# The scan of an RWKV-7 layer: a step's values with the direction outermost, and two neighbouring chunks side by side in the blocks of L

## Chip and metric

One core of a Trainium2 chip runs the whole program, one launch. The metric is the device time of one execution in microseconds; it is given as the median of three runs. Engines are named as in the profile: PE (TensorE), DVE (VectorE), ACT (ScalarE), POOL (GpSimd) and SP (SyncE), from whose queue nearly all DMAs are issued.

## What is computed

Two layers of a diffusion backbone over 512 latent and 256 context tokens with 1024 channels. The change lies in layer 1, whose mixer is a bidirectional RWKV-7: 16 heads of 64 channels, each with a 64 x 64 state that is carried along the tokens once forwards and once backwards, first over the context, then over the latent tokens.

```python
def wkv_scan(r, w, kk, bvec, k, v, s0, reverse):
    def step(s, inp):
        r_t, w_t, kk_t, b_t, k_t, v_t = inp
        sk = jnp.einsum('bhvk,bhk->bhv', s, kk_t)
        s = s * w_t[:, :, None, :] - sk[..., None] * b_t[:, :, None, :] + v_t[..., None] * k_t[:, :, None, :]
        return s, jnp.einsum('bhvk,bhk->bhv', s, r_t)
    ...
for d, rev in enumerate((False, True)):
    s_c, y_c = wkv_scan(rc, dc[d][0], kkc, dc[d][1], dc[d][2], vc, s0, rev)
    _, y_l = wkv_scan(rl, dl[d][0], kkl, dl[d][1], dl[d][2], vl, s_c, rev)
```

## The kernel before

The tokens are cut into 12 chunks of 64 (8 latent, 4 context). The kernel works chunk by chunk: within a chunk the recurrence is solved with a 64 x 64 triangular matrix L per head and direction, whose inverse is applied to the right-hand sides, and only the state passes from chunk to chunk. A step `i` of the scan (`tm_scan`, 12 steps) takes one chunk of the forward direction and one of the backward direction, listed in `order`: forwards the chunk number rises by one from step to step, backwards it falls by one. The two directions lie in the two halves of the 128 partitions (`half`), so nearly every load of the scan fills 64 partitions. Heads are counted as 8 tiles `kt` of 2 heads `n`.

Before the scan, `tm_prep` has written to HBM the keys (`kbd`), queries (`qld`, `qcd`) and the blocks of L (`ld`, with 64 columns a chunk, all 12 chunks of a row side by side), and `tm_values` the values (`vd`, one row of 4 KB per token).

`tm_feed(i)` loads what step `i` needs: four loads of keys KB (256 KB each), two of queries QZ (512 KB each, 256 KB for context), and two of values W (256 KB each, one per direction, L1071). It then makes G = QZ x KB on PE, masks it on DVE (L1082), and transposes KB on PE (L1096). `tm_feed(i + 1)` is a generator of which one part runs after each `kt` of step `i`. KB has room for one step only, so the next KB loads wait for the transposes; QZ and W have room for two steps.

`tm_invert(j)` serves steps 2j and 2j + 1: it loads their blocks of L into the tile XT (four loads of 256 KB, L1111), copies the triangles into GL with a mask (four copies, L1114, DVE), transposes GL into Z (L1118) and inverts the 32 x 32 blocks by a row of small products on DVE or POOL (L1124, L1125). `tm_below(j)` transposes the result into XN and XD (L1133, L1134) and completes the inverse on PE; ACT writes it back into XT in place (L1148, L1156). XT has three buffers, so pairs 0, 1 and 2 are loaded before the scan and pairs 3, 4 and 5 when an earlier pair has been used, at the ends of steps 1, 3 and 5.

`tm_step(i, kt)` multiplies W with G, applies the inverse from XT, writes the solution into W through a mask (L1182), and multiplies it with the transposed keys into the new state S (L1194). After four `kt` the state is copied into the W of the next step (L1200).

Each engine works its instructions in order, and so does each DMA queue. The order is not that of the code: the program is built with `TileContext(nc, schedule_with_timeline_sim=True)`, a planner that places each engine's instructions by estimates of their durations and adds the waits between engines by which parts of a tile they read and write. After the scan `out1_ahead` uses buffers of XT for weights (L1359).

Of the kernel before, what the change touches and what calls it, by code (L numbers as in the profile page):

```python
# [7 lines left out]
F32 = mybir.dt.float32  # L8
F32R = mybir.dt.float32r
I32 = mybir.dt.int32  # L10
AF = mybir.ActivationFunctionType
# [4 lines left out]
P = 128  # L16
D = 1024
KT = 8
# [16 lines left out]
class Net:  # L35
# [1014 lines left out]
    half = staticmethod(lambda n: slice(64 * n, 64 * n + 64))  # L1050

    def tm_feed(self, i, KB=None, W=None):

        nc, half = self.nc, self.half
        f = self.feeds[i] = {}
        cs = self.order[i]
        lat = cs[0] < 8
        m = 128 if lat else 64
        KB = KB or [self.sb([P, 4, 2, 128], F32, "KB", 2) for _ in range(2)]
        W = f["W"] = W or self.sb([P, KT, 2, 2, 64], F32, "W", 2)  # L1060
        QZ = f["QZ"] = self.QZ[i % 2]
        by = lambda z: z.rearrange("k (n p) m -> p (k n) m", n=2)
        flat = lambda z: z.rearrange("p k n m -> p (k n) m")
        for d in range(2):
            h = half(1 - d)
            for g in range(2):
                nc.sync.dma_start(flat(KB[g][h]), by(self.kbd[d, 4 * g:4 * g + 4, :, cs[d]]))
            nc.sync.dma_start(flat(QZ[h, :, :, d, 0:m]), by(self.qld[d, :, :, cs[d]] if lat else self.qcd[d, :, :, cs[d] - 8]))
        for d in range(2):
            v = self.vd[64 * cs[d]:64 * cs[d] + 64].rearrange("t (k n v) -> t k n v", n=2, v=64)  # L1070
            nc.sync.dma_start(W[half(d), :, d], v)  # L1071
        f["G"], f["KT"] = [], []
        yield
        for g in range(4):
            ps = self.mm2()
            for j in range(2):
                for n in range(2):
                    x = 2 * m * (2 * j + n)
                    self.mm(ps[:, x:x + 2 * m], KB[g // 2][:, 2 * (g % 2) + j, n], QZ[:, 2 * g + j, n, :, 0:m], True, True)
            G = self.sb([P, 2, 2, 2, m], F32, "G", 8)  # L1080
            f["G"].append(G)
            nc.vector.tensor_mul(G.rearrange("p k n d t -> p (k n) d t"),  # L1082
                                 ps[:, :8 * m].rearrange("p (k d t) -> p k d t", d=2, t=m),
                                 self.gmask[:, :, 0:m].unsqueeze(1).to_broadcast([P, 4, 2, m]))
            if i:

                for d in range(2):
                    h = half(1 - d)
                    nc.scalar.activation(G[h, :, :, d, 0:64], QZ[h, 2 * g:2 * g + 2, :, d, 0:64], AF.Copy)
            yield  # L1090
        for g in range(2):
            ps = self.mm2()
            for j in range(4):
                for n in range(2):
                    x = 256 * j + 128 * n
                    nc.tensor.transpose(ps[:, x:x + 128], KB[g][:, j, n], self.ident)  # L1096
            T = self.sb([P, 4, 2, 128], F32, "KT", 3, pool=self.gp)
            nc.scalar.activation(T, ps.rearrange("p (k n x) -> p k n x", k=4, n=2), AF.Copy)
            f["KT"].append(T)
            yield  # L1100

    def tm_invert(self, j):


        nc = self.nc
        XT = self.XT[j] = self.sb([P, 2, 2, KT, 64], F32, "XT", 3, pool=self.ip)
        for s in range(2):
            for d in range(2):
                c = self.order[2 * j + s][d]
                h = self.half(1 - d)  # L1110
                nc.sync.dma_start(XT[h, s].rearrange("p n k t -> p (n k) t"),  # L1111
                                  self.ld[:, :, h, 64 * c:64 * c + 64].rearrange("n k p t -> p (n k) t"))
            for b in range(2):
                nc.vector.copy_predicated(self.GL[:, 16 * s:16 * s + 16],  # L1114
                                          self.pmask[:, b].unsqueeze(1).to_broadcast([P, 16, 32]),
                                          XT[:, s, :, :, 32 * b:32 * b + 32].rearrange("p n k t -> p (n k) t"))
        Z = self.Z[j] = self.sb([P, 32, 32], F32, "Z", 2, pool=self.ip)
        nc.vector.transpose(Z, self.GL.rearrange("p u t -> p t u"))  # L1118
        zt = self.sb([P, 256], F32, "zt", 2)
        eng = nc.gpsimd if j in self.pool_inverse else nc.vector  # L1120
        for u in range(1, 31):
            n = 31 - u
            t = zt[:, 0:n * u].rearrange("p (a b) -> p a b", b=u)
            eng.tensor_mul(t, Z[:, u + 1:, u:u + 1].to_broadcast([P, n, u]), Z[:, u:u + 1, 0:u].to_broadcast([P, n, u]))  # L1124
            eng.tensor_add(Z[:, u + 1:, 0:u], Z[:, u + 1:, 0:u], t)  # L1125

    def tm_below(self, j):

        nc, Z = self.nc, self.Z[j]
        XA = self.XT[j]  # L1130
        XT = XA.rearrange("p s n k t -> p (s n k) t")
        XD, XN = (self.sb([P, 32, 32], F32, n, 1, pool=self.ip) for n in ("XD", "XN"))
        nc.vector.transpose(XN.rearrange("p u t -> p t u"), Z.rearrange("p t s -> p s t"))  # L1133
        nc.vector.transpose(XD.rearrange("p u t -> p t u"), Z)  # L1134
        units = lambda z: z.rearrange("p (n k) t -> p n k t", n=2)
        for s in range(2):
            us = slice(16 * s, 16 * s + 16)
            pp = self.mm2()[:, :512].rearrange("p (u t) -> p u t", t=32)
            for u in range(16):
                for h in (0, 64):  # L1140
                    self.mm(pp[h + 32:h + 64, u], XT[h:h + 32, 16 * s + u, 32:64], XN[h:h + 32, 16 * s + u], True, True)
            PL = self.sb([P, 16, 32], F32, "PL", 2, pool=self.ip)
            for h in (32, 96):
                nc.scalar.activation(PL[h:h + 32], pp[h:h + 32], AF.Copy)
            for d, z in ((0, XD), (1, XN)):
                h = self.half(1 - d)
                for b in range(2):
                    nc.scalar.activation(XA[h, s, :, :, 32 * b:32 * b + 32], units(z[h, us]), AF.Copy, scale=self.bmask[h, b:b + 1])  # L1148
            yield
            pp = self.mm2()[:, :512].rearrange("p (u t) -> p u t", t=32)  # L1150
            for u in range(16):
                for h, d in ((0, 1), (64, 0)):
                    x, y = PL[h + 32:h + 64, u], XD[h + 32:h + 64, 16 * s + u]
                    self.mm(pp[h + 32 * d:h + 32 * d + 32, u], *((y, x) if d else (x, y)), True, True)
            for d, h in ((0, 64), (1, 32)):
                nc.scalar.activation(XA[h:h + 32, s, :, :, 32 - 32 * d:64 - 32 * d], units(pp[h:h + 32]), AF.Copy)  # L1156
            yield

    def tm_step(self, i, kt):

        nc, half, order = self.nc, self.half, self.order
        f, cs = self.feeds[i], order[i]
        lat, first, last = cs[0] < 8, i == 0, i == len(order) - 1
        g, j = kt // 4, kt % 4
        W = f["W"][:, kt]
        XT = self.XT[i // 2][:, i % 2]
        Q = f["QZ"][:, kt]
        G = f["G"][kt // 2][:, kt % 2]
        K = f["KT"][g][:, j]
# [1 line left out]
        units = [(d, n) for n in range(2) for d in range(2)]  # L1171
# [6 lines left out]
        nc.scalar.activation(rh, pr[:, 0:128].rearrange("p (n v) -> p n v", n=2), AF.Copy)  # L1178
        for d, n in units:
            h = half(1 - d)  # L1180
            self.mm(pr[h, col(1, n)], XT[h, n, kt], rh[h, n], True, True)
        nc.vector.copy_predicated(W, self.umask.unsqueeze(2).unsqueeze(3).to_broadcast([P, 2, 2, 64]),  # L1182
                                  pr[:, 128:256].rearrange("p (n v) -> p n v", n=2).unsqueeze(1).to_broadcast([P, 2, 2, 64]))
        if not last:
# [11 lines left out]
            if j == 3:  # L1196
                W2 = self.feeds[i + 1]["W"]
                for d in range(2):
                    h = half(1 - d)
                    nc.scalar.activation(W2[h, 4 * g:4 * g + 4, d], self.S2[h], AF.Copy)  # L1200
            if j == 3 and i < len(order) - 2:
                m = self.dec[:, :, 4 * g:4 * g + 4, i + 1].rearrange("p n k -> p k n")
                self.Sd[g] = self.sb([P, 4, 2, 64], F32, "Sd", 3, pool=self.gp)
# [72 lines left out]
    def tm_scan(self):  # L1276
# [5 lines left out]

        qz = lambda j: self.sb([P, KT, 2, 2, 128], F32, "QZ%d" % j)
        q = qz(0)
        ahead = [self.sb([P, 4, 2, 128], F32, "KB", 2) for _ in range(2)], self.sb([P, KT, 2, 2, 64], F32, "W", 2)
        self.QZ = [q, qz(1)]
        for j, z in enumerate(self.QZ):
            for d in range(2):
# [2 lines left out]
        n, below = len(self.order), iter(())  # L1291
# [56 lines left out]
    def out1_ahead(self):  # L1348

        nc, a = self.nc, self.a  # L1350
        gs = self.sb([P, 32, 32], F32, "Z", 2, pool=self.ip).rearrange("p a b -> p (a b)")
        nc.sync.dma_start(gs, a["rw_gup"])
        st = [self.sb([P, 2, 2, KT, 64], F32, "XT", 3, pool=self.ip) for _ in range(2)]
        self.ahead = gs, [z.rearrange("p a b c d -> p (a b c d)").rearrange("p (k n) -> p k n", n=256) for z in st]
        for c in range(2):
            self.load_wo(self.ahead[1][c], c)
# [171 lines left out]
```

## Time and profile before

| | us |
|---|---|
| median of 3 runs | 2261.82 |
| lowest and highest of the runs | 2259.23, 2261.92 |
| the profiled execution | 2269.31 |
| its span, first to last instruction | 2267.5 |

The profile is of one execution, all of whose times are counted from the first instruction of its span. The scan with the inversions ahead of it lies between about 1375 and 1820 us. The page gives the engines' shares; the views by stretch, the waits and the timelines go into single stages. In a row, `XT<-ldr` is a load of the tile XT from the HBM tensor ldr, and `mm<-QZ,KB` a product of QZ and KB into a PSUM tile. A packet is one piece of a DMA on one of 16 DMA engines.

### The profile page before, as it was taken

The numbers are of one execution on the slowest core, as the hardware profiler recorded it, in microseconds if no ns is written. First come the engines' busy times: TensorE is split into PE (matmuls) and PEld (weight loads), VectorE is DVE, ScalarE is ACT, GpSimd is POOL, SyncE is SP. The second block draws the span as 40 slices with busy tenths as digits, with TensorE's granted clock in tenths as the row PEclk, the third lists the DMA queues.
The fourth block names the chain that finished last, engine by engine and source line by source line (L and its number), as shares of the span: only waits on it lengthen the run. The fifth ranks groups of instructions, "written<-read, shape, count | busy, mean of one in ns | idle before, by whom it ended". The sixth has DMA issues, their size and how long they took to land. (4 is left out here: it accounts for less than half of the span.)

```text
span 2267.5 us, 37320 instructions
## 1 busy us (share of the span) xinstructions
PE 2023.4 (89%) x15710; PEld 1619.3 (71%) x15710; DVE 1145.4 (51%) x1835; ACT 869.6 (38%) x1333; POOL 519.6 (23%) x530
## 2 busy tenths in 40 slices
PE   5888889999999999997987769779787778999999
PEld 3666547778888888875765449667676666888887
DVE  4556664342222222328647997648575684333333
ACT  3664454231121221317744543346454432232321
POOL 0122331010010100105004983661500220110110
PEclk8999999999999999998998778889898999999999
DMA  7324441123333122212224659396644440222222
GB/s 282 119 86 136 143 164 41 37 94 119 124 129 113 56 64 67 98 42 79 93 88 148 236 223 214 71 143 102 113 91 80 76 140 19 93 93 93 93 93 93
DMA packets 231944, 248.93 MB, mean 110 GB/s; under 512 B 52448, under 2 KB 209504, under 8 KB 225376
## 3 DMA queue, kind: packets, MB, share of 16 engines
q1 hardware_dynamic: 229728, 241.30, 36.8%
q0 software_dynamic: 896, 3.15, 0.4%
q8 instruction: 123, 2.02, 0.4%
q10 hardware_dynamic: 1152, 2.10, 0.2%
q14 instruction: 45, 0.37, 0.1%
HBM read 200.82 MB, written 41.94 MB: 107 GB/s over the span
## 5 line engine op out<-in xcount | busy, mean ns | idle before, releaser
L264 ACT ACTIVATE whi<-wst 128x1024 fp32r<-128x1024 f32 x160 | 169.2, 1059 | 587.3 <-PE mm L47 567.0
L47 PE MATMUL mm<-hhi,whi 128*128 128x512 f32 (+1 forms) x992 | 346.8, 356 | 16.2 <-ACT hhi L250 6.7
L47 PE MATMUL mm<-hlo,whi 128*128 128x512 f32 (+1 forms) x992 | 352.0, 356 | 3.6 <-DVE hlo L251 3.4
L47 PE MATMUL mm<-hhi,wlo 128*128 128x512 f32 (+1 forms) x992 | 349.6, 353 | 0.0
L265 DVE TENSOR_TENSOR wlo<-wst,whi 128x1024 fp32r<-128x1024 f32 x160 | 199.9, 1251 | 255.2 <-ACT whi L264 252.4
L345 POOL TENSOR_TENSOR mp<-mr 128x768 f32<-128x768 f32 (+1 forms) x64 | 109.9, 1719 | 848.1 <-ACT mr L344 848.1
L47 PE MATMUL mm<-ahi,wlo 128*128 128x512 f32 (+1 forms) x704 | 252.9, 359 | 0.0
L47 PE MATMUL mm<-ahi,whi 128*128 128x512 f32 (+1 forms) x704 | 252.9, 360 | 0.0
L47 PE MATMUL mm<-alo,whi 128*128 128x512 f32 (+1 forms) x704 | 252.5, 359 | 0.0
L300 DVE SCALAR_TENSOR_TENSOR Xt<-mm,mod,Xt 128x512 f32<-128x512 f32 (+1 forms) x112 | 70.6, 653 | 336.8 <-PE mm L47 336.6
L47 PEld LDWEIGHTS mm<-hhi,whi 128*128 128x128 f32 x992 | 187.8, 191 | 55.2 <-ACT hhi L250 8.7
L47 PEld LDWEIGHTS mm<-hlo,whi 128*128 128x128 f32 x992 | 188.9, 190 | 32.1 <-DVE hlo L251 6.6
L47 PEld LDWEIGHTS mm<-hhi,wlo 128*128 128x128 f32 x992 | 188.4, 190 | 28.3 <-issue 0.8
L47 PEld LDWEIGHTS mm<-ahi,whi 128*128 128x128 f32 x704 | 132.2, 188 | 28.1 <-issue 6.7
L47 PEld LDWEIGHTS mm<-ahi,wlo 128*128 128x128 f32 x704 | 132.5, 188 | 22.0 <-DVE wlo L265 1.1
L47 PEld LDWEIGHTS mm<-alo,whi 128*128 128x128 f32 x704 | 132.4, 188 | 21.9
L47 PE MATMUL mm<-QZ,KB 128*128 128x256 f32 (+1 forms) x384 | 96.4, 408 | 48.1 <-DMA QZ<-qlr 20.3
L47 PEld LDWEIGHTS mm<-QZ,KB 128*128 128x128 f32 x384 | 74.1, 227 | 60.3 <-issue 26.3
L347 DVE TENSOR_TENSOR alo<-mp,ahi 128x768 fp32r<-128x768 f32 (+1 forms) x64 | 54.9, 858 | 113.1 <-ACT ahi L346 113.0
L1082 DVE TENSOR_TENSOR G<-mm,gmask 128x1024 f32<-128x1024 f32 (+1 forms) x48 | 50.2, 1047 | 88.1 <-PE mm L47 87.8
L346 ACT ACTIVATE ahi<-mp 128x768 fp32r<-128x768 f32 (+1 forms) x64 | 47.3, 739 | 110.3 <-POOL mp L345 110.3
L47 PE MATMUL sc<-W,G 128*64 128x64 f32 (+1 forms) x1280 | 67.8, 233 | 12.8 <-DVE S L1194 10.3
(462 smaller groups left out, 4207.7 us busy)
## 6 DMA issues: line engine op xcount, KB each, us to landing
wst<-in_mlp_w_dram SPq DMA_DIRECT2D x64, 1024.0 KB, 5.4
wst<-in_ada_w_dram SPq DMA_DIRECT2D x48, 1024.0 KB, 6.4
kbr<-KB SPq DMA_DIRECT2D x16, 768.0 KB, 4.5
KB<-kbr SPq DMA_DIRECT2D x48, 256.0 KB, 5.6
wst<-in_rw_w_rkv_dram SPq DMA_DIRECT2D x8, 1024.0 KB, 5.4
qlr<-ql SPq DMA_DIRECT2D x16, 512.0 KB, 3.3
QZ<-qlr SPq DMA_DIRECT2D x16, 512.0 KB, 8.8
wst<-in_hy_w_in_dram SPq DMA_DIRECT2D x7, 1024.0 KB, 5.3
```

Of the source, the lines that this page charges most:

```text
L47: self.nc.tensor.matmul(out, lhsT, rhs, start=start, stop=stop)
L264: nc.scalar.activation(hi, w, AF.Copy)
L265: nc.vector.tensor_sub(lo, w, hi.bitcast(F32))
L300: self.nc.vector.scalar_tensor_tensor(x, ps[:, c0:c1], self.m(l, chunk, v, kt), x, op0=OP.mult, op1=OP.add)
L345: nc.gpsimd.tensor_mul(p[:, :n], r[:, :n], r[:, :n])
L346: nc.scalar.activation(h[:, :n], p[:, :n], AF.Copy)
L347: nc.vector.tensor_sub(o[:, :n], p[:, :n], h[:, :n].bitcast(F32))
L1082: nc.vector.tensor_mul(G.rearrange("p k n d t -> p (k n) d t"), ps[:, :8 * m].rearrange("p (k d t) -> p k d t", d=2, t=m), self.gmask[:, : ...
```

## The change

W has its axes as direction, `kt`, head, value in place of `kt`, direction, head, value. A direction's values of one token are then 4 KB in one piece in the tile as well as in HBM, where the load before had 8 pieces of 512 B.

XT has its axes as head, `kt`, chunk of the pair, column in place of chunk, head, `kt`, column. A pair's two chunks are neighbours in HBM, so one load per direction brings both, in pieces of 128 columns (512 B) in place of 64 (256 B): two loads of 512 KB in place of four of 256 KB. Place `s` in a tile is now the lower or higher chunk rather than the earlier or later step: the earlier step finds its chunk at place 0 for the forward and at place 1 for the backward direction (`at`). The four copies into GL each read a place of both loads. The instructions on the engines are the same in number and size; their strides differ. The tiles are as large as before.

```diff
@@ tm_feed
-        W = f["W"] = W or self.sb([P, KT, 2, 2, 64], F32, "W", 2)
+        W = f["W"] = W or self.sb([P, 2, KT, 2, 64], F32, "W", 2)
         for d in range(2):
-            v = self.vd[64 * cs[d]:64 * cs[d] + 64].rearrange("t (k n v) -> t k n v", n=2, v=64)
-            nc.sync.dma_start(W[half(d), :, d], v)
+            nc.sync.dma_start(W[half(d), d].rearrange("p k n v -> p (k n v)"), self.vd[64 * cs[d]:64 * cs[d] + 64])
@@ tm_invert
-        XT = self.XT[j] = self.sb([P, 2, 2, KT, 64], F32, "XT", 3, pool=self.ip)
+        XT = self.XT[j] = self.sb([P, 2, KT, 2, 64], F32, "XT", 3, pool=self.ip)
+        for d in range(2):
+            c = min(self.order[2 * j][d], self.order[2 * j + 1][d])
+            h = self.half(1 - d)
+            nc.sync.dma_start(XT[h].rearrange("p n k s t -> p (n k) (s t)"),
+                              self.ld[:, :, h, 64 * c:64 * c + 128].rearrange("n k p t -> p (n k) t"))
         for s in range(2):
-            for d in range(2):
-                c = self.order[2 * j + s][d]
-                h = self.half(1 - d)
-                nc.sync.dma_start(XT[h, s].rearrange("p n k t -> p (n k) t"),
-                                  self.ld[:, :, h, 64 * c:64 * c + 64].rearrange("n k p t -> p (n k) t"))
             for b in range(2):
                 nc.vector.copy_predicated(self.GL[:, 16 * s:16 * s + 16],
                                           self.pmask[:, b].unsqueeze(1).to_broadcast([P, 16, 32]),
-                                          XT[:, s, :, :, 32 * b:32 * b + 32].rearrange("p n k t -> p (n k) t"))
+                                          XT[:, :, :, s, 32 * b:32 * b + 32].rearrange("p n k t -> p (n k) t"))
@@ tm_below
-            us = slice(16 * s, 16 * s + 16)
+            at = s, 1 - s
...
-                    nc.scalar.activation(XA[h, s, :, :, 32 * b:32 * b + 32], units(z[h, us]), AF.Copy, scale=self.bmask[h, b:b + 1])
+                    nc.scalar.activation(XA[h, :, :, at[d], 32 * b:32 * b + 32], units(z[h, 16 * at[d]:16 * at[d] + 16]), AF.Copy,
+                                         scale=self.bmask[h, b:b + 1])
...
@@ tm_step
-        W = f["W"][:, kt]
-        XT = self.XT[i // 2][:, i % 2]
+        W = f["W"][:, :, kt]
+        XT = [self.XT[i // 2][:, :, :, (i + d) % 2] for d in range(2)]
...
-                    nc.scalar.activation(W2[h, 4 * g:4 * g + 4, d], self.S2[h], AF.Copy)
+                    nc.scalar.activation(W2[h, d, 4 * g:4 * g + 4], self.S2[h], AF.Copy)
```

## Rows read from the trace of the kernel before

**Rows 1.** the page: busy time, share of the span, instructions of PE
```profile
PE 2023.4 (89%) x15710; PEld 1619.3 (71%) x15710; DVE 1145.4 (51%) x1835; ACT 869.6 (38%) x1333; POOL 519.6 (23%) x530
```

**Rows 2.** stretches: length, busy us per engine, clock, DMA share, GB/s
```profile
1375.00:1464.00 89.00, 73.42 (x801) 72.24 (x801) 64.32 (x87) 22.17 (x30) 45.55 (x70) 0.89 0.56 116
1464.00:1820.00 356.00, 287.45 (x5315) 244.24 (x5314) 221.65 (x552) 173.16 (x369) 106.96 (x152) 0.89 0.60 103
```

**Rows 3.** waits, 1464 to 1820: total us, times, longest
```profile
PE mm L47 <- DMA QZ<-qlr: 20.3, 4, 7.8
...
DVE GL L1114 <- DMA XT<-ldr: 14.5, 5, 5.3
...
PE mm L47 <- DMA KB<-kbr: 6.8, 4, 2.8
```

**Rows 4.** timeline of PE: start, us, instruction, [idle before, what ended it]
```profile
1441.53 0.69 PE L47 MATMUL mm<-XN,XT 32*32 32x32 f32 x18 [14.27 <-DVE XN L1133]
...
1523.74 1.62 PE L47 MATMUL mm<-QZ,KB 128*128 128x128 f32 x6 [0.28 <-DMA KB<-kbr]
...
1542.64 1.19 PE L47 MATMUL mm<-QZ,KB 128*128 128x256 f32 x2 [2.81 <-DMA KB<-kbr]
...
1635.73 0.58 PE L47 MATMUL sc<-W,G 128*64 128x64 f32 x5 [4.53 <-DVE S L1194]
...
1743.28 0.79 PE L47 MATMUL mm<-QZ,KB 128*128 128x256 f32 x1 [7.80 <-DMA QZ<-qlr]
...
1778.28 1.19 PE L47 MATMUL mm<-QZ,KB 128*128 128x256 f32 x2 [8.10 <-issue]
```

**Rows 5.** timeline of SP's queue: start and us of the issues
```profile
1379.14 9.71 SPq L1111 DMA_DIRECT2D XT<-ldr  x7
...
1511.76 1.50 SPq L1111 DMA_DIRECT2D XT<-ldr  x2
1513.37 4.49 SPq L1067 DMA_DIRECT2D KB<-kbr  x2
...
1731.12 0.52 SPq L1071 DMA_DIRECT2D W<-vdr  x1
1731.73 1.74 SPq L1068 DMA_DIRECT2D QZ<-qlr  x2
...
1767.64 3.06 SPq L1067 DMA_DIRECT2D KB<-kbr  x2
```

**Rows 6.** timeline of DVE: the copies into GL
```profile
1383.24 1.52 DVE L1114 COPY_PREDICATED GL<-pmask,XT 128x512 f32<-128x512 int32 x2 [4.35 <-DMA XT<-ldr]
1387.88 1.52 DVE L1114 COPY_PREDICATED GL<-pmask,XT 128x512 f32<-128x512 int32 x2 [3.12 <-DMA XT<-ldr]
...
1634.59 0.73 DVE L1114 COPY_PREDICATED GL<-pmask,XT 128x512 f32<-128x512 int32 x1 [5.32 <-DMA XT<-ldr]
...
1645.93 0.73 DVE L1114 COPY_PREDICATED GL<-pmask,XT 128x512 f32<-128x512 int32 x1 [4.17 <-DMA XT<-ldr]
```

**Rows 7.** DMA, 1728 to 1745: packets, MB, share of 16 engines
```profile
q1 hardware_dynamic: 5248, 2.62, 92.2%
```

**Rows 8.** DMA, 1380 to 1389, XT loads
```profile
q1 hardware_dynamic: 5172, 1.30, 93.4%
```

**Rows 9.** DMA, 1030.8 to 1035, one load into 128 partitions; GB/s by slice
```profile
GB/s 0 0 0 0 0 0 0 0 0 0 93 171 215 180 88 39 73 34 24 68 190 351 327 351 351 351 351 341 356 346 332 225 102 29 5 0 0 0 0 0
...
q1 hardware_dynamic: 1040, 0.52, 41.9%
```

**Rows 10.** DMA, 1511.0 to 1511.3: issues, KB, us to landing
```profile
QZ<-qlr SPq DMA_DIRECT2D x1, 512.0 KB, 5.5
```

**Rows 11.** tile XT: count, ns min/median/max, first and last start
```profile
L1148 ACT ACTIVATE XT<-XN,bmask x24: 704/722/725, 1441.6 to 1788.0; 64x512 f32<-64x512 f32 x24
```

**Rows 12.** tile bo, 1816 to 1822
```profile
L1233 SPq DMA_DIRECT2D bo<-vdr x4: 524/628/970, 1816.3 to 1818.6; - x4
...
DMA to landing us min/median/max: 2.6/2.9/3.1
```

More of the change, by code (lines that the diff above doesn't have):

```diff
@@ L1130, in tm_below @@
         XA = self.XT[j]
-        XT = XA.rearrange("p s n k t -> p (s n k) t")
+        XT = XA.rearrange("p n k s t -> p (n k) s t")
         XD, XN = (self.sb([P, 32, 32], F32, n, 1, pool=self.ip) for n in ("XD", "XN"))
@@ L1136, in tm_below @@
         for s in range(2):
-            us = slice(16 * s, 16 * s + 16)
+            at = s, 1 - s
             pp = self.mm2()[:, :512].rearrange("p (u t) -> p u t", t=32)
             for u in range(16):
-                for h in (0, 64):
-                    self.mm(pp[h + 32:h + 64, u], XT[h:h + 32, 16 * s + u, 32:64], XN[h:h + 32, 16 * s + u], True, True)
+                for h, d in ((0, 1), (64, 0)):
+                    self.mm(pp[h + 32:h + 64, u], XT[h:h + 32, u, at[d], 32:64], XN[h:h + 32, 16 * at[d] + u], True, True)
             PL = self.sb([P, 16, 32], F32, "PL", 2, pool=self.ip)
@@ L1152, in tm_below @@
                 for h, d in ((0, 1), (64, 0)):
-                    x, y = PL[h + 32:h + 64, u], XD[h + 32:h + 64, 16 * s + u]
+                    x, y = PL[h + 32:h + 64, u], XD[h + 32:h + 64, 16 * at[d] + u]
                     self.mm(pp[h + 32 * d:h + 32 * d + 32, u], *((y, x) if d else (x, y)), True, True)
             for d, h in ((0, 64), (1, 32)):
-                nc.scalar.activation(XA[h:h + 32, s, :, :, 32 - 32 * d:64 - 32 * d], units(pp[h:h + 32]), AF.Copy)
+                nc.scalar.activation(XA[h:h + 32, :, :, at[d], 32 - 32 * d:64 - 32 * d], units(pp[h:h + 32]), AF.Copy)
             yield
@@ L1180, in tm_step @@
             h = half(1 - d)
-            self.mm(pr[h, col(1, n)], XT[h, n, kt], rh[h, n], True, True)
+            self.mm(pr[h, col(1, n)], XT[d][h, n, kt], rh[h, n], True, True)
         nc.vector.copy_predicated(W, self.umask.unsqueeze(2).unsqueeze(3).to_broadcast([P, 2, 2, 64]),
@@ L1284, in tm_scan @@
         q = qz(0)
-        ahead = [self.sb([P, 4, 2, 128], F32, "KB", 2) for _ in range(2)], self.sb([P, KT, 2, 2, 64], F32, "W", 2)
+        ahead = [self.sb([P, 4, 2, 128], F32, "KB", 2) for _ in range(2)], self.sb([P, 2, KT, 2, 64], F32, "W", 2)
         self.QZ = [q, qz(1)]
@@ L1352, in out1_ahead @@
         nc.sync.dma_start(gs, a["rw_gup"])
-        st = [self.sb([P, 2, 2, KT, 64], F32, "XT", 3, pool=self.ip) for _ in range(2)]
+        st = [self.sb([P, 2, KT, 2, 64], F32, "XT", 3, pool=self.ip) for _ in range(2)]
         self.ahead = gs, [z.rearrange("p a b c d -> p (a b c d)").rearrange("p (k n) -> p k n", n=256) for z in st]
```

## The prediction

> **What bounds the kernel now.** I read the page first: PE is busy for 89% of the span [rows 1], so only a stage in which PE waits can be changed much by loads. The table by stretches finds it: from 1464 to 1820 us (the scan) PE is busy 287 of 356 us, and in the 89 us before it (values and first inversions) 73 of 89 [rows 2]. Everything that the diff touches lies in these two stretches. The list of waits in the scan names what PE and DVE sit idle for: the loads QZ 20.3 us, KB 6.8 us, and, on DVE, XT 14.5 us [rows 3]. The loads of W themselves hardly appear; they matter by standing in SP's queue ahead of QZ, KB and XT. The timeline of PE then shows single waits: 14.27 us for XN before the scan, and inside it 2.81 us where a step's KB load comes first in the queue, 7.80 us where QZ comes last, 8.10 us where KB comes last [rows 4]. SP's timeline gives the order of issue behind these waits [rows 5], and DVE's the copies into GL that wait for XT [rows 6].
>
> **What a piece costs.** Three windows of the DMA view give the time of a packet as share x 16 engines x length / packets. Into 64 partitions, pieces of 512 B (KB, QZ, W): 0.922 x 16 x 17.0 us / 5248 = 47.8 ns [rows 7]. Into 64 partitions, pieces of 256 B (XT): 0.934 x 16 x 9.0 / 5172 = 26.0 ns [rows 8]. Into 128 partitions, pieces of 512 B (a weight load): 0.419 x 16 x 4.2 / 1040 = 27.1 ns, with a plateau of 350 GB/s [rows 9]. So the same 512 B cost 1.8 times as much when a load fills half of the partitions. In rates over 16 engines the half-width loads run at 157 GB/s with 256 B and 171 GB/s with 512 B: doubling the piece gave 9%, and the width costs most of the rest. This is the row on which I differ from the change's own words: W and XT stay half-width loads.
>
> **W.** 24 loads of 256 KB, from 512 pieces of 512 B to 64 of 4 KB. Now: 512 x 47.8 / 16 = 1.53 us of all engines. After, no row shows 4 KB into half of the partitions. Bounds: 1.53 us (width alone decides; no reason puts it above) and 262144 B / 350 GB/s = 0.75 us (piece alone decides). Value: three more doublings at 9% each, 171 x 1.29 = 220 GB/s, 1.2 us, nearest to the half-width row; saved 0.3 us a load. Most of this lies beside other work: on the path are loads queued ahead of something that PE or DVE waits for. I count nine: the first of the pair ahead of QZ at 1594, 1696 and 1731 us (the last of these in [rows 5] with its QZ), both ahead of KB at 1763 to 1768, both ahead of the last XT at 1565, and both ahead of the scan's first side loads at 1465 (the last place in [rows 5]). 9 x 0.3 = 2.7 us saved, bounds 0 and 9 x 0.78 = 7.0.
>
> **XT before the scan.** Six pairs of chunks, four loads of 256 KB each become two of 512 KB, pieces 256 B to 512 B: 2 x 1024 x 26.0 / 16 = 3.33 us becomes 1024 x 47.8 / 16 = 3.06, only 8% less; half as many issues on SP. For the first pair, DVE starts two copies at 1383.24, waits 3.12 us and starts the other two at 1387.88, done 1389.4 [rows 6]. After, all four copies need both loads. The second load can't be issued before 1379.14, as the dec loads stand ahead [rows 5], and a 512 KB half-width load alone lands 5.5 us after its issue [rows 10]: 1384.6, plus four copies of 0.76 makes 1387.7, so 1.7 us earlier. DVE is busy nearly without a break from there to XN, on which PE waits 14.27 us [rows 4], so this reaches the scan's start. 1.7 us saved, bounds 0 (DVE put in another order) and 3.0 (under A below).
>
> **XT inside the scan,** three times (pairs 3, 4, 5), each when the pair's buffer is freed. At 1511 two XT loads stand ahead of the KB loads, two behind [rows 5]. If the two new loads keep the first places, 2 x 256 KB more pass ahead of KB, at 200 GB/s 2.6 us; PE started the matmuls on that KB 0.28 us after its last wait [rows 4], so up to 2.6 us show; I take 2, as the second XT load may slip behind KB (bounds -0.5 and 2.6 + 1.5 for two more copies on DVE ahead of S). At 1564 KB goes first and XT's last load comes some 0.5 us sooner: -0.5 (bounds -1.5, 1.5). At 1622 to 1637 DVE waits 5.32 us for the second XT load, and PE 4.53 us behind it for S [rows 4, 6]; with both loads twice as long that is 2.6 us later, but the fourth load, which held DVE 4.17 us at 1645.93 [rows 6], is gone: about 1 us lost (bounds -1.5, 4). Sum: 2.5 us lost, bounds -3.5 and 9.6.
>
> **Engines.** The same instructions with other strides on ACT, DVE and PE; every innermost run stays 32 or more elements. The copies that change are GL (0.73 us) and, on ACT, the masked writes to XT and the state into W; ACT is busy half of the scan [rows 2], so a few per cent on them are hidden. At zero; if the cover were gone, 5% of 48 masked writes of 0.72 us [rows 11] would be 1.7 us.
>
> **Sum.** 2.7 + 1.7 - 2.5 = 1.9 us saved. The profiled execution took 2269.31 us around its span of 2267.5; the median of the three runs is 2261.82, 7.5 us less. I take the difference over to the median: 2259.9 us. A measurement of this kernel can tell about 0.2% (4.5 us) from no change, so this is no difference that can be told.
>
> **Rivals.**
> A, the piece is the bound. If it is the many small descriptors and not the width that hold the half-width loads at 171 GB/s, W saves 0.75 us at nine places (6.8), an XT load of 512 KB costs 1024 x 27.1 / 16 = 1.73 us, as much as 256 KB now, so nothing is delayed at 1511 and 1622 (1.5 saved there), and the start gains 1.7 + 1.3 = 3.0: 11.3 us, 2250.5 us. For it: whole-width loads with 512 B reach 350 GB/s. Against it: that these do, with the same piece.
> A2, XT alone gains. If it is only the 256-byte pieces that run below the rate, XT as under A and W at nothing: 3.0 + 1.5 = 4.5 us saved, 2257 us. Against it: 157 and 171 GB/s are nearly the same rate [rows 7, 8]. [...]
> B, slower: XT arrives as one lump. Both loads must be there before the first copy, DVE works in order, and S and W for the running step stand behind the copies. At 1511 and 1622 each 2.6 us for the longer loads plus 1.5 for two more copies in a row, 8.2 together, less 1 of W and 1 at the start: 6.2 us lost, 2268 us. It decides once DVE's first copy for pair 3 starts over 2 us later than now behind the same step. For it: 5.32 us of DVE waiting for XT in a single place [rows 6]. Against: half of the traffic is behind the copies now and could be hidden.
> C, another order. The program is put in order by a planner's estimate of durations, and the estimates of W and XT change. What an order is worth stands in [rows 4]: KB last in the queue 8.10 us of PE, KB first 2.81, so 5.3 us for a step, of either sign: 2255 or 2265 from the forecast.
> D, the loads are still cut into 512 B: then W gains nothing, 2262 us. Little speaks for it; a row of W is 4 KB on both sides.
> E, chunks of a pair now lie in alternating stripes of XT. If the writes for one chunk held the reads of the other, five pairs would each wait for four masked writes on ACT, 4 x 0.72 = 2.9 us [rows 11], 14 us in all: 2274 us. Against: four loads into alternating stripes of bo were all issued before the first had landed, 2.6 us at the least [rows 12], so stripes aren't held for one another.
>
> **How the numbers follow.** Forecast 0.39 (of it 0.30 within 0.2%, 0.09 faster; own range 2255 to 2265), A 0.21 (faster), A2 0.05 (0.03 faster, 0.02 same), B 0.20 (slower), C 0.10 (0.02 faster, 0.04 same, 0.04 slower), D 0.03 (same), E 0.02 (slower). Faster 0.35, same 0.39, slower 0.26. The range reaches into A to 2248 and past B to 2270; what is left out is A's far end and E.
>
> **What would show it.** Right: packets of 4 KB for W and none of 256 B for XT; the rate in the scan still near 200 GB/s where half-width loads alone are in flight; XN some 2 us earlier behind the values; QZ's waits shorter by 0.3 us, not by 0.8; a longer wait of DVE for XT at pair 3. Wrong by A: a rate over 300 GB/s while W is moved, and QZ's waits down by a microsecond each. Wrong by B: copies into GL ending PE's waits through S. Wrong by C: KB, QZ and W issued in another order at the heads of the steps.

## The result, and the profile after

| | before | changed |
|---|---|---|
| median, us (4 runs each) | 2260.53 | 2281.6 |
| lowest and highest | 2258.43, 2261.92 | 2280.7, 2285.76 |
| ratio, 95% interval | | 1.0098 (1.008 to 1.0115) |
| the profiled execution | 2269.31 | 2281.89 |
| its span | 2267.5 | 2280.1 |

The change makes the kernel some 21 us slower; a second timing, on another occasion, gave 1.0090 (1.0071 to 1.0108). The forecast was 2259.9 us, no difference that can be told, with a range up to 2270: the time lies outside it. The two profiled executions differ by only 12.6 us, because that of the kernel before was itself 8.8 us above the median of these runs. So a trace of a run with W's new layout alone, whose instructions stand in the same order as before on every engine, is used below as a second base; its profiled execution took 2261.24 us.

The page (PE's line), and the table by stretches with the scan's start moved to 1468.5 us (length, busy us per engine, clock, DMA share, GB/s), answer to [rows 1, 2]:

```profile
PE 2026.2 (89%) x15710; PEld 1623.2 (71%) x15710; DVE 1143.8 (50%) x1835; ACT 868.7 (38%) x1333; POOL 521.7 (23%) x530
...
1375.00:1468.50 93.50, 76.99 (x805) 75.53 (x804) 62.97 (x88) 22.97 (x32) 45.52 (x69) 0.87 0.53 111
1468.50:1832.00 363.50, 280.48 (x5249) 239.18 (x5248) 219.22 (x551) 170.57 (x366) 103.70 (x152) 0.88 0.55 101
```

PE has the same work (2026 against 2023 us) and the granted clock is within 0.02 of before in both stretches: what has grown is idle time. The waits from 1468.5 to 1832 us (total, times, longest) answer to [rows 3]:

```profile
PE mm L47 <- DMA KB<-kbr: 27.8, 6, 8.6
...
PE mm L47 <- issue: 20.3, 4, 7.4
...
DVE GL L1114 <- DMA XT<-ldr: 15.1, 3, 8.5
...
PE mm L47 <- DMA QZ<-qlr: 5.3, 1, 5.3
...
PE sc L47 <- DVE W L1183: 4.9, 3, 3.9
```

The totals for XT hardly differ (15.1 us in 3 waits for 14.5 in 5). The single waits do. PE's timeline (start, us, instruction, idle before and what ended it) answers to [rows 4]; `wvl` is the low part of the weight `wv`, which DVE splits off:

```profile
1409.47 0.58 PE L47 MATMUL mmb<-wvl,vxh 128*128 128x256 f32 x1 [2.23 <-DVE wvl L368]
1433.58 0.58 PE L47 MATMUL mmb<-wvl,vxh 128*128 128x256 f32 x1 [5.40 <-DVE wvl L368]
1444.10 0.32 PE L47 MATMUL mm<-XN,XT 32*32 32x32 f32 x4 [8.87 <-DVE XN L1133]
1530.27 0.55 PE L47 MATMUL mm<-QZ,KB 128*128 128x128 f32 x1 [6.99 <-DMA KB<-kbr]
1608.08 0.38 PE L47 MATMUL sc<-W,KT 128*64 128x64 f32 x2 [3.93 <-DVE W L1183]
1620.26 0.80 PE L47 MATMUL mm<-QZ,KB 128*128 128x256 f32 x1 [5.27 <-DMA QZ<-qlr]
1653.97 0.38 PE L47 MATMUL sc<-W,G 128*64 128x64 f32 x2 [7.59 <-DVE S L1195]
```

Three of these stand out: for wvl ahead of the scan (7.6 us in two waits; W alone has one, of 2.76), for the values W at the end of the fifth step (step 4, as steps are counted from 0; in the table below this wait counts for step 5), and for a QZ load that SP issued only at 1611.49. SP's queue, answering to [rows 5]:

```profile
1515.96 1.49 SPq L1110 DMA_DIRECT2D XT<-ldr  x2
1517.55 5.18 SPq L1067 DMA_DIRECT2D KB<-kbr  x2
...
1610.93 0.47 SPq L1070 DMA_DIRECT2D W<-vdr  x1
1611.49 1.29 SPq L1068 DMA_DIRECT2D QZ<-qlr  x2
...
1640.94 1.57 SPq L1110 DMA_DIRECT2D XT<-ldr  x2
```

And DVE's timeline, the copies into GL answering to [rows 6], with what stands in front of the waits above:

```profile
1387.08 2.61 DVE L1114 COPY_PREDICATED GL<-pmask,XT 128x512 f32<-128x512 int32 x4 [7.37 <-DMA XT<-ldr]
...
1402.51 1.85 DVE L1114 COPY_PREDICATED GL<-pmask,XT 128x512 f32<-128x512 int32 x2 [3.81 <-DMA XT<-ldr]
...
1407.13 2.28 DVE L368 TENSOR_TENSOR wvl<-wv,wvh 128x2048 fp32r<-128x2048 f32 x1
...
1527.21 1.33 DVE L1114 COPY_PREDICATED GL<-pmask,XT 128x512 f32<-128x512 int32 x2 [5.28 <-DMA XT<-ldr]
...
1603.90 2.03 DVE L1133 STREAM_TRANSPOSE XN<-Z 128x1024 f32<-128x1024 f32 x1
1605.84 1.91 DVE L1134 STREAM_TRANSPOSE XD<-Z 128x1024 f32<-128x1024 f32 x1
1607.62 1.07 DVE L1183 COPY_PREDICATED W<-umask,sc 128x256 f32<-128x256 int32 x3
...
1652.22 1.33 DVE L1114 COPY_PREDICATED GL<-pmask,XT 128x512 f32<-128x512 int32 x2 [8.48 <-DMA XT<-ldr]
```

At 1402.51 DVE stops for the third pair's L blocks with the split of wv queued behind (PE's waits for wvl follow); at 1603.90 the two transposes XN and XD stand ahead of three copies into W (PE's 3.93 us follow). In the trace of W alone both stand the other way round:

```profile
1398.47 2.31 DVE L368 TENSOR_TENSOR wvl<-wv,wvh 128x2048 fp32r<-128x2048 f32 x1
1401.14 0.96 DVE L1113 COPY_PREDICATED GL<-pmask,XT 128x512 f32<-128x512 int32 x1
...
1593.82 0.44 DVE L1181 COPY_PREDICATED W<-umask,sc 128x256 f32<-128x256 int32 x1
...
1595.55 2.06 DVE L1132 STREAM_TRANSPOSE XN<-Z 128x1024 f32<-128x1024 f32 x1
```

Of the 96 copies into W in the scan, 44 stand ahead of this XN there, and 39 in the changed kernel. This is another order of instructions, and it is the planner's: the program with two XT loads a pair in place of four is ordered differently on all five engines, on DVE from the second pair's copies into GL on. With W's layout alone every engine keeps the order of before in the trace. With both new layouts and still four loads the planner keeps it too; that program was built but not run, so no time stands beside it.

Lengths of stages make runs comparable whose starts differ (the first XT load is issued 2.9 us later in this trace than in that of W alone, after the same work). A step's length is taken from ACT's first copy rh of a step to that of the next (96 copies, eight a step); the last step ends with PE's last product of S and QZ, and Z is the transpose of GL. The fourth and fifth columns hold runs that are told further down. In us:

| stage | before | W alone | larger loads, old order | new order in steps 4, 5 only | changed |
|---|---|---|---|---|---|
| first Z to step 0 | 77.7 | 78.6 | 77.0 | 77.0 | 82.1 |
| steps 0, 1 | 45.5 | 44.2 | 45.1 | 45.4 | 45.0 |
| step 2 | 21.4 | 21.3 | 23.1 | 24.4 | 26.7 |
| step 3 | 29.9 | 28.7 | 29.0 | 28.7 | 27.0 |
| step 4 | 27.3 | 27.3 | 28.7 | 30.4 | 29.9 |
| step 5 | 34.5 | 34.0 | 32.4 | 40.4 | 40.1 |
| step 6 | 27.2 | 26.6 | 28.2 | 28.0 | 34.7 |
| step 7 | 38.2 | 38.4 | 37.6 | 37.4 | 30.7 |
| steps 8 to 11 | 125.3 | 123.6 | 123.0 | 123.1 | 122.2 |
| behind the scan | 451.1 | 450.6 | 450.4 | 450.4 | 452.1 |

Against W alone the changed kernel loses 3.5 us ahead of the scan, 3.7 in steps 2 and 3, 8.7 in steps 4 and 5, 0.4 in steps 6 and 7 (8.1 lost, 7.7 given back), and 0.9 in the rest.

### The profile page after: what moved, and what is told of

Same layout as the page of the kernel before. It is cut to its first block, busy times and chain, and to the rows that moved or that the text cites. A ratio compares the mean times of both kernels' runs of the same rounds, so it can differ in the third digit from the quotient of the medians.

```text
span 2280.1 us, 37289 instructions
## 1 busy us (share of the span) xinstructions
PE 2026.2 (89%) x15710; PEld 1623.2 (71%) x15710; DVE 1143.8 (50%) x1835; ACT 868.7 (38%) x1333; POOL 521.7 (23%) x530
## 5 line engine op out<-in xcount | busy, mean ns | idle before, releaser
L47 PEld LDWEIGHTS mm<-QZ,KB 128*128 128x128 f32 x384 | 74.2, 227 | 68.6 <-issue 40.6
```

The lines of the kernel that those rows point to most:

```text
L47: self.nc.tensor.matmul(out, lhsT, rhs, start=start, stop=stop)
```

## Experiments

To tell loads from order, kernels were made that hold each engine to a written order. `ORDER` lists, per engine, the places of the instructions in the program as traced; a dependency without a semaphore is put between neighbours:

```diff
         net.run(out)
+        pin(tc, nc, net.loads)
...
+        for x, y in zip(row, row[1:]):
+            tc.add_manual_dep(y, x.name, info, reason="order")
```

"Old order" is that of the kernel before, "new order" that of the changed kernel. In the old order a 512 KB load stands where the first of the two small loads of its direction stood. Medians are against runs of the kernel before on the same occasion.

### Loads or order: four runs

**W alone.** The W edits of the diff, nothing else.

> The kernel before with the new layout of W alone; every engine has the instruction order of the kernel before. Theory 1 (the loss of some 21 us comes from the order that the planner makes once the L blocks are loaded by two loads a pair): no loss here, 0 to 3 us faster than before, 2258 to 2261 us. Theory 2 (the two larger loads themselves, as lumps ahead of the keys and of the first copy, cost the time): the same 0 to 3 us. Theory 3 (the W loads in pieces of 4 KB disturb loads beside them): slower by 5 us or more, above 2265 us.

2262.78 us beside 2263.52, ratio 0.9993 (0.9983 to 1.0002). No loss: theory 3 falls. The gain of 1.6 us by the ratio is inside the noise (0.7 by the medians).

**XT alone.** The XT edits of the diff, W as before.

> The changed kernel with W's old layout: the two larger loads of L blocks a pair and their new order alone. Theories 1 and 2: slower than before by about as much as the changed kernel, 2279 to 2285 us. Theory 3: close to before, under 2270 us.

2287.75 us, ratio 1.0100 (1.0085 to 1.0115). The XT edits, with their two loads a pair, carry the whole loss.

**Both layouts, two loads, old order.**

> The changed kernel with both layouts and the two larger loads a pair, but with every engine's instructions held in the order of the kernel before (a larger load stands where the first pair of small ones stood). Theory 1 (the order): within 5 us of before, 2256 to 2266 us. Theory 2 (the lumps): the loss stays, 2275 us or more. Between them, each has a part in proportion.

2266.33 us, ratio 1.0012 (1.0002 to 1.0022): 2.7 us in place of 21. Theory 2 falls as the main cause. DVE's and PE's timelines of this run:

```profile
1382.41 2.94 DVE L1116 COPY_PREDICATED GL<-pmask,XT 128x512 f32<-128x512 int32 x4 [7.45 <-DMA XT<-ldr]
...
1517.84 0.73 DVE L1116 COPY_PREDICATED GL<-pmask,XT 128x512 f32<-128x512 int32 x1 [5.37 <-DMA XT<-ldr]
```

```profile
1518.88 0.37 PE L47 MATMUL sc<-W,G 128*64 128x64 f32 x2 [5.29 <-DVE S L1197]
...
1633.94 0.37 PE L47 MATMUL sc<-W,G 128*64 128x64 f32 x2 [8.01 <-DVE S L1197]
```

The larger loads do make DVE stop longer with S behind (PE's 8.01 us stand against 4.53 before [rows 4]), but step 6 grows by only 1.0 us against before and 1.6 against W alone. Part of the difference is the next wait: behind it PE stood 0.99 us for queries before (1.06 with W alone), and no longer does.

**Both layouts, four small loads, new order.**

```diff
-        for d in range(2):
-            c = min(self.order[2 * j][d], self.order[2 * j + 1][d])
...
         for s in range(2):
+            for d in range(2):
+                c = min(self.order[2 * j][d], self.order[2 * j + 1][d]) + s
+                h = self.half(1 - d)
+                nc.sync.dma_start(XT[h, :, :, s].rearrange("p n k t -> p (n k) t"),
+                                  self.ld[:, :, h, 64 * c:64 * c + 64].rearrange("n k p t -> p (n k) t"))
```

> Both layouts, but the L blocks come by four loads of 256 KB a pair as before (pieces of 256 B), and every engine's instructions are held in the order of the changed kernel (the second small load of a direction right behind the first). Theory 1 (the order): nearly the whole loss, 2277 to 2285 us. Theory 2 (the lumps): the loads of a pair still come all ahead of the keys in this order, so the difference to the changed kernel is only that of a load's packets; then this run and the one in the old order both lose, this one 2270 us or more and that one 2275 us or more.

2289.04 us, ratio 1.0108 (1.0095 to 1.0121), a little above the range of theory 1. With the old loads and the new order all of the loss is there; with the new loads and the old order 2.7 us of it. The order is the cause.

### Where in the order: prelude, scan, and its halves

The two orders hold the same instructions up to the scan's first masks on every engine, so they can be joined there. All with both layouts and two loads a pair.

> The changed kernel (both layouts, two larger loads a pair) with every engine held in the order of the changed kernel up to the scan's first masks, and in the order of the kernel before from there on. Theory P (the order ahead of the scan has its own part, since the third pair's copies into GL stand ahead of the split of wv on DVE): from Z to the scan's start some 4.5 us longer than in the old order, 3 to 6 us above the run that is wholly in the old order, 2268 to 2273 us. Theory S (all of the loss is made in the scan): within 2 us of that run, 2264 to 2268 us.

2269.34 us, ratio 1.0024 (1.0012 to 1.0036), against 1.0012 wholly in the old order: some 2.7 us, though the two intervals overlap; from Z to step 0 the trace has 81.2 us, 4.3 more. That is near the lower end of theory P (3 us), and the stage bears it out.

> The other half: the order of the kernel before up to the scan, that of the changed kernel from there on, both layouts and two larger loads a pair. Theory P: the changed kernel less the part ahead of the scan, 2277 to 2283 us. Theory S: as slow as the changed kernel on this chip, 2283 to 2290 us.

2281.95 us, ratio 1.0076 (1.0060 to 1.0092): most of the loss is made in the scan.

> The changed kernel with every engine in the order of the changed kernel for the scan's steps 0 to 5 only, and in that of the kernel before ahead of the scan and from step 6 on. From the stages, steps 2 to 5 are some 10 us longer in the new order and the rest some 5: theory 5 (the loss sits mostly in steps 2 to 5): 2272 to 2278 us. Rival (it is the end of the scan, steps 6 to 11): 2265 to 2270 us.

2279.32 us, ratio 1.0069 (1.0053 to 1.0086), a little above the range of theory 5. Steps 0 to 5 carry nearly all of the scan's part.

The last cut, early in step 4, goes by what each engine had started at that time in the trace.

> The changed kernel with every engine in the order of the kernel before, but from the scan's start to the first product with the keys of step 5's successor (early in step 4) in the order of the changed kernel. Theory 23 (the loss in the scan comes from the fourth pair's four copies and loads in steps 2 and 3): 2274 to 2280 us. Theory 45 (it comes from the ends of steps 4 and 5): 2265 to 2270 us, since the stages show only some 2 us more in steps 2 and 3 than the run in the old order.

2269.13 us, ratio 1.0017 (1.0005 to 1.0029). Step 2 is 27.0 us long, about as in the changed kernel (26.7), but step 3 gives 2 us back.

> The complement: the order of the kernel before up to that place early in step 4, the order of the changed kernel from there to the end of step 5, then that of the kernel before again. Theory 45: 2273 to 2278 us, with PE waiting for W behind XN and XD, and then for queries, in step 5. Theory 23: 2265 to 2269 us.

2276.76 us, ratio 1.0054 (1.0039 to 1.0068), 4.2 thousandths or 9.5 us above the old order: theory 45. This is the largest single part.

> The changed kernel as it is, once more, on the chip of the other three: 19 to 26 us slower than before, 2280 to 2288 us; the base for the sum of the parts (3 us ahead of the scan, 14 in steps 0 to 5, 2 from step 6 on, 3 for the larger loads themselves, -1 for W).

2286.1 us beside 2265.58, ratio 1.0090 (1.0071 to 1.0108). In thousandths: larger loads in the old order 1.2, prelude 1.2, steps 0 to 3 0.5, steps 4 and 5 4.2, steps 6 on 0.7 (1.0076 less 1.0069); together 7.8 of 9.0, the rest within the intervals.

### What in steps 4 and 5

The trace of the run with the new order in steps 4 and 5 shows a chain. The waits of SP's own queue, then DVE's, PE's and SP's timelines:

```profile
SPq L1071 <- DVE W L1185: 10.1, 1, 10.1
```

```profile
1598.97 2.00 DVE L1135 STREAM_TRANSPOSE XN<-Z 128x1024 f32<-128x1024 f32 x1
1600.85 1.89 DVE L1136 STREAM_TRANSPOSE XD<-Z 128x1024 f32<-128x1024 f32 x1
1602.59 1.09 DVE L1185 COPY_PREDICATED W<-umask,sc 128x256 f32<-128x256 int32 x3
```

```profile
1603.08 0.37 PE L47 MATMUL sc<-W,KT 128*64 128x64 f32 x2 [3.96 <-DVE W L1185]
1615.28 0.79 PE L47 MATMUL mm<-QZ,KB 128*128 128x256 f32 x1 [6.66 <-DMA QZ<-qlr]
```

```profile
1605.92 0.47 SPq L1071 DMA_DIRECT2D W<-vdr  x1
1606.49 1.29 SPq L1069 DMA_DIRECT2D QZ<-qlr  x2
```

DVE's copies into W, the first of them the last of step 4, stand behind XN and XD; SP's next load of W needs the buffer that this copy and the product behind it release, and the queries' loads stand behind it in SP's queue. This W load is issued 15.9 us after the first KB load of the same step's feed (7.0 us in the old order). Two attempts undid parts of it.

```diff
 DVE
-XN XD (fourth pair)
 W W W W S ... S
+XN XD (fourth pair)
 ACT
-XT<-XN XT<-XN
 rh
-XT<-XD XT<-XD
 W<-S W<-S Y Y Y Y
+XT<-XN XT<-XN XT<-XD XT<-XD
```

> As the run with the new order in the scan alone, but of it one thing put back: in the fifth step (step 4) the two transposes XN and XD of the fourth pair and ACT's four masked writes behind them stand behind that step's last value updates instead of ahead of them. Theory Q (these two transposes, 3.9 us of DVE, hold the last W of the step, by that PE for 3.9 us, by that the buffers of W and QZ and so the next loads of QZ, for which PE waits 5.3 us): steps 4 and 5 together 6 to 9 us shorter, 2270 to 2276 us. Rival (the next wait behind takes it, for KB, QZ or the last pair's load): 0 to 3 us shorter, 2276 to 2282 us.

2279.33 us, ratio 1.0063 (1.0048 to 1.0078), 1.3 thousandths less than without the moves: the rival. PE's wait for W goes, and its wait for queries in step 5 grows from 5.76 to 6.71 us; steps 4 and 5 together go from 68.5 to 66.3 us.

```diff
 DVE
 S (step 4)
+W (last of step 4)
 zt Z zt Z XN XD
-W (last of step 4)
```

> As s45 (new order in steps 4 and 5 only), but one single instruction moved on DVE: the last copy into W of step 4 stands ahead of the last zt and Z products and of XN and XD of the fourth pair, instead of behind them (5 to 9 us of DVE work). Theory D (that copy holds the release of W's buffer, by that the W load in SP's queue, for 10.1 us, and the queries' loads behind it): these loads are issued some 8 us sooner, PE's 6.7 us for queries go, 6 to 9 us faster than s45, 2266 to 2271 us where s45 had 2277. Rival (the buffers are held by something else too, PE's other wait of 4 us takes over): 0 to 3 us, 2273 to 2277 us.

2276.76 us, ratio 1.0057 (1.0042 to 1.0072). Theory D falls: nothing is gained, and steps 4 and 5 together take 71.3 us for 70.8. SP's waits, then PE's and ACT's timelines of this run, say why:

```profile
SPq L1071 <- PE sc L47: 7.8, 1, 7.8
SPq L1071 <- DVE W L1185: 5.9, 1, 5.9
```

```profile
1605.21 0.37 PE L47 MATMUL sc<-rh,XT 64*64 64x64 f32 x2 [4.66 <-ACT rh L1181]
```

```profile
1603.66 1.33 ACT L1150 ACTIVATE XT<-XN,bmask 64x512 f32<-64x512 f32 x2 [4.25 <-DVE XN L1135]
1604.90 0.25 ACT L1181 ACTIVATE rh<-sc 128x128 f32<-128x128 f32 x1
```

DVE now gives W early, but ACT's next copy rh stands behind its masked writes, which wait for XN, and PE stands at the product with that rh, with the last readers of step 4's buffers behind it. The same decision, XN ahead of the step, is written into three queues, and moving one instruction in one of them exchanges the wait for another.

> The changed kernel in its own order throughout, with that one copy moved. Theory D: 6 to 9 us faster than the changed kernel, 2276 to 2280 us. Rival: 0 to 3 us, 2282 to 2286 us.

2285.74 us, ratio 1.0096 (1.0078 to 1.0114): the same in the changed kernel's own order. Beside the changed kernel as planned (1.0090 and 1.0098) it also says that holding an order by dependencies costs nothing that can be told.

So steps 4 and 5 are shown to carry the largest part, and the inversion's end ahead of the step's end is shown to be a place that PE waits at. That it accounts for all of the 9.5 us isn't shown: with XN, XD and ACT's writes put back together, 66.3 us remain against 61.1 in the old order. Which further moves in the row of small products zt and Z would close that gap was not tried.

### A version that beats both

**Small loads inside the scan only.** Old order, W's layout, 512 KB loads for the three pairs ahead of the scan.

```diff
+        for s in range(1 if j < 3 else 2):
+            for d in range(2):
+                at = s if d == 0 else 1 - s
...
```

> The order of the kernel before throughout, W's new layout, the larger loads of L blocks for the three pairs ahead of the scan, four small loads each for the three pairs inside it. From the stages of the run in the old order with larger loads (the first copies start at once, steps 2, 4 and 6 each 1.4 to 1.7 us longer by the lumps): 1 to 4 us faster than before, 2259 to 2263 us. If the lumps cost nothing: as the old-order run, 2264 to 2268 us.

2281.38 us, ratio 1.0071 (1.0055 to 1.0087), a miss by the edit itself: the small loads came by step (`at`), while the copies read by place, so the first copy needed the first and the fourth load. It shows how long DVE stops at a copy that waits for the last load of a pair; DVE's timeline at the fourth pair:

```profile
1530.57 0.73 DVE L1122 COPY_PREDICATED GL<-pmask,XT 128x512 f32<-128x512 int32 x1 [14.58 <-DMA XT<-ldr]
```

Step 2 became 32.6 us long. With `at = s`:

> As the run with larger loads for the three pairs ahead of the scan and small ones inside it, in the order of the kernel before, but the small loads of the fourth to sixth pair bring the chunks by place in the tile, as the copies read them (there they came by step, so that the first copy waited for the fourth load). If that was the whole loss of that run: waits of DVE for the first copies back at 3 to 6 us, 2257 to 2263 us. If small loads into the striped layout cost something themselves (stripes held for one another): above 2268 us.

2261.96 us, ratio 0.9995 (0.9985 to 1.0004). Writing neighbouring stripes of XT costs nothing that can be measured (rival E falls), and the larger loads ahead of the scan bring nothing that can be measured.

**L blocks later.** Two places in SP's queue and two in DVE's, in the old order:

```diff
 SP, steps 2 and 6
-XT XT
 KB KB ... W (step 6: QZ QZ W)
+XT XT
 DVE, steps 2 and 6
-GL
 S ... S
-GL
 ...
+GL GL
 GL ... GL
```

> The changed kernel (both layouts, two larger loads a pair) in the order of the kernel before, with two moves: the loads of the fourth and of the sixth pair of chunks stand behind the keys, values and (sixth pair) queries of their step in SP's queue, and on DVE their first two copies into GL stand next to the last two. Theory L (what a pair's larger loads cost inside the scan is that they stand ahead of keys and queries, and that DVE stops at the copies with S behind them): in steps 2 and 6 the waits of PE for S, 5.3 and 8.0 us in the run in the old order, go; some of it is taken by the waits for keys and queries behind; 6 to 12 us faster than that run, 2253 to 2260 us, faster than before. Rival (the next load in the queue takes it all, since the bytes are the same): 0 to 3 us, 2263 to 2267 us.

2262.6 us, ratio 0.9998 (0.9987 to 1.0009), 1.4 thousandths or 3.2 us better than the old order alone: short of theory L and at the edge of the rival; the two intervals overlap a little. Step 2 fell from 23.1 to 17.5 us as expected, step 3 and 4 gave back 2.8, and in step 6 DVE stopped 9.93 us for the loads at the later place too.

> The same two moves in the same order, but the L blocks come by four loads of 256 KB a pair in pieces of 256 B into the new layout. If the larger piece has a worth of its own (1.7 us ahead of the scan, 8% shorter transfers): 1 to 4 us slower than the same with larger loads. If it has none: within 1 us of it.

2259.85 us, ratio 0.9982 (0.9968 to 0.9996): not slower but, if anything, faster than with the larger loads (3.6 us by the ratios, outside both expectations; the intervals overlap). The larger piece has no worth of its own here.

> As the run with four small loads a pair that come later and copies put together, but in step 6 the four copies of the sixth pair and its transpose Z stand on DVE behind the masks and updates of that step and behind XN of the fifth pair. If DVE's stop at these copies is what PE still waits for in step 6 (2.9 us for the mask G): 1 to 4 us faster than that run, 2255 to 2259 us. If the queries' loads are late anyway (3.3 us): within 1 us of it.

2260.65 us beside 2265.58, ratio 0.9981 (0.9970 to 0.9992): 4.3 us faster than before (W's new layout has a part in it that isn't told apart), and some 25 faster than the changed kernel on that occasion. DVE's copies of the sixth pair no longer wait:

```profile
1640.43 2.88 DVE L1116 COPY_PREDICATED GL<-pmask,XT 128x512 f32<-128x512 int32 x4
```

Step 6 fell from 27.0 to 20.8 us, and step 7 took 3.2 of that back (43.4 for 40.2). Against the run before it the ratio is the same: what was gained there isn't told from noise.

## Why the prediction was wrong, point by point

**W: the price of a load right, its worth on the path not told.** In the changed kernel's trace the 20 W loads from 1480 us on have 1280 packets of 4 KB, which took 307 ns on average, 64 x 307 / 16 = 1.23 us a load; the forecast was 1.2. In the queue a W load adds 1.11 us to the landing of the load ahead of it, with W alone as in the changed kernel, for 1.36 before (medians of 20 places): 0.25 us saved where 0.3 was said. The sum of 2.7 us lies in the measured interval of W alone, which reaches from 3.8 us faster to 0.5 slower; so does zero.

**XT before the scan: mis-sized.** 1.7 us saved was forecast. In the old order, from the first XT load's issue to Z took 13.9 us, for 14.0 before and 12.8 with W alone: nothing. The step that failed is the second load's landing. The 5.5 us were read from a load alone [rows 10]; here it landed 6.52 us after its issue (1375.81 to 1382.33), and that issue came 4.3 us after the first one (3.7 before). It shared the DMA engines with the small pieces of the dec loads ahead of it (44 B each, moving until 1377) and with the next pair's loads behind it; which of the two held it isn't shown.

**XT inside the scan: about right in kind and size, for the order that was assumed.** In the old order step 2 grew by 1.8 us against W alone (2 lost was forecast), steps 4 and 5 together shrank by 0.2 (28.7 + 32.4 against 27.3 + 34.0; 0.5 less was forecast), and steps 6 and 7 grew by 0.8 (1 lost was forecast). A 512 KB load adds 2.9 us to the queue, for 2 x 1.62 before, 10% less (8% forecast). With the order held, the whole forecast came out 2.7 us above before instead of 1.9 below. The missing 1.7 us ahead of the scan are part of that; how the rest divides between W and noise isn't told.

**Engines: right.** In the changed kernel the copies into GL take 729 ns (median; 738 before) and ACT's masked writes 716 (722 before [rows 11]).

**Rival C: this is where the forecast failed.** The step that failed is that the sum takes every engine's order as kept: a change of order stands in it at nothing. As a rival it was named, with a chance of 0.10, but priced as one wait of one step (5.3 us of either sign), and its sign was to be another order of issue at the heads of the steps in SP's queue. That sign came, at the head of step 3 and from step 7 on, but not in steps 4 and 5, where most is lost. The runs show in its place an order that differs on five engines from the prelude to the scan's end and costs some 18 us: 2.7 ahead of the scan, 9.5 in steps 4 and 5, the rest spread. The places that decided were in DVE's and ACT's queues (pair 3's copies ahead of wvl, XN and XD ahead of W and rh), which no single load wait shows. The cause named, that the estimates of W and XT change, was half wrong: W's estimate changes nothing in the order, nor does XT's layout; two loads for four do. Why the planner then orders as it does stays open.

**A and A2 fell.** 4 KB x 16 / 307 ns is 213 GB/s, not over 300. PE's three long waits for queries, 5.98, 5.54 and 7.80 us before, are 6.01, 5.07 and 7.78 with W alone (the second ended by a load of W there): none is down by a microsecond. A 512 KB load of XT adds 2.9 us to the queue, where A and A2 had 1.73. **B** was right in its mechanism (the copies end PE's waits through S, 5.29 and 8.01 us in the old order, 2.92 and 4.53 before) and too high in price: 8.2 us was said for the two places, and steps 2 and 6 grew by 3.4 in all against W alone. **D** and **E** fell: pieces of 4 KB, no more 256 B pieces of XT, and no cost of striped writes.

Of the signs given, pieces, rate and the longer wait of DVE at the fourth pair (5.28 us in the changed kernel, 3.00 before) came as said; the 0.3 us less at each wait for queries did not show. Counted from the first XT load's issue, XN came 1.7 us later (65.8 for 64.1) instead of 2 earlier; the order ahead of the scan had changed.

## What to carry to other kernels

Where a planner orders the program, a change in the number of instructions may be a change of the whole order; price that as many waits and not as one (the new order cost some 18 us here, where PE sat idle for 68.6 of the scan's 356 us [rows 2]), and hold the order fixed before a time is put down to a transfer. Compare the two orders engine by engine: look for work that isn't needed soon (an inversion for two steps later) in front of the step's own updates, in every queue that it passes. A load that is needed late goes behind those needed soon, and the copy that waits for it behind the updates that others wait for; here such moves gained some 3 us in the old order, if anything, and the larger pieces of XT nothing.

## What was not expected of the hardware

- In these traces the size of the piece counted for less than the width in loads into 64 partitions: 256 B ran at 157 GB/s and 512 B at 171 [rows 7, 8], 4 KB at 213 (307 ns a packet, on average among other loads, the two loads for the two halves standing close together in the queue), against 350 with 512 B into 128 partitions [rows 9]. What sets these rates isn't shown.
- Two W loads for the two halves, with next to nothing else in flight (128 packets from 1464.97 to 1467.24 us in the changed kernel), moved 0.52 MB at 231 GB/s, 8% above the 213 of the W loads in the scan. No run shows the rate of a single W load alone, so what a pair gains over one load isn't told.
- A gain or a loss in a step was taken back by the next, in large part: step 6 lost 8.1 us and step 7 gave 7.7 back in the changed kernel, and 6.2 gained in step 6 cost 3.2 in step 7 in the last version.
